# Loads that carry both experts of a pair, a first gather in one piece, and a re-ordered last pair in a one-core mixture-of-experts layer

## Chip, core and metric

The kernel runs on one core of one Trainium2 chip. The metric is device time in microseconds (us) of one execution. The kernel before takes 1322.36 us, the median of three runs (1322.08 to 1322.64).

## What is computed

One encoder layer on 256 tokens of width 2048, all in float32. The first part (an input projection, a gated convolution, a differential attention and an output projection) stays as it is. The second part is a mixture of 32 experts, of which each token uses two of the eight in one group:

```python
def hier_moe(x, w_group, b_group, w_router, b_router, w_gate, w_up, w_down):
    ...
    expert_id = g_idx[:, None] * EXPERTS_PER_GROUP + top_i
    combine = jnp.sum(jax.nn.one_hot(expert_id, N_EXPERTS, dtype=jnp.float32)
                      * (g_w * top_p)[..., None], axis=1)
    out = jnp.zeros_like(t)
    for e in range(N_EXPERTS):
        h = jax.nn.silu(t @ w_gate[e]) * (t @ w_up[e])
        out = out + combine[:, e:e + 1].astype(t.dtype) * (h @ w_down[e])
    return out.reshape(B, S, D)
...
        h = h + jnp.concatenate([y_conv, y_attn], axis=-1) @ w_out[l]
        h = h + hier_moe(rms_norm(h, norm2_g[l]), ...)
```

The gate and up matrices of an expert are 2048 x 512 each, the down matrix is 512 x 2048. The 32 experts hold 403 MB of the 466 MB that the kernel reads from HBM.

## The kernel before

The tokens of an expert are brought together in 64 slots, and two experts make a pair: 16 pairs, `p` = 0 to 15, NP = 16. The helpers below are those of the page's lines.

- `dispatch` (L836) makes the 0/1 matrix `dg` of a pair on VectorE. `gather` (L855) multiplies the tokens `xs` with `dg` on TensorE (L861) for n blocks of 128 features and scales the result into `tT` on VectorE (L863). `tT` has 16 blocks, so a pair takes four gathers of four blocks.
- `gate_up` (L869) multiplies `tT` of one expert with its eight chunks of gate and up weights (L880), into one PSUM bank of the two called "gu"; then comes the silu on ScalarE (L884) and the product `hid` on VectorE (L885). It runs for the one expert of the pair and then for the other (`gate_ups`, L1010).
- `flip_hidden` (L887) turns `hid` into `hT` (TensorE L891, ScalarE L893). `down` (L904) makes 512 output columns of both experts (L909), four times a pair; the four results stay in the PSUM banks called "dn". `flip_weights` (L896) turns `dg` into `dwT`.
- `weigh` (L916) splits a down result into a high and a low part `y` (ScalarE L926, VectorE L927). `scatter` (L931) multiplies `y` with `dwT` (L939) and adds it to the accumulators `acc` (L940). The scatter of pair p-1 stands in the loop of pair p, between the gathers of pair p+1. In the last loop (p = 15) there are no gathers any more, and the scatter of pair 14 stands alone ahead of the downs of pair 15. Behind them each down's scatter and the stores follow.
- A sum in float32 is two passes on TensorE: each matmul with float32 operands has two records in the trace (16 records are eight matmuls).

**Loads.** All weights come through the SP queue in items of 2 MiB, in the order in which they are used: per pair eight items of gate and up (`("gu", p, j)`: two chunks of one expert each) and four of down (`("dn", p, n)`: 512 columns of both experts). There are 192 items. They go round a ring of nine buffers, `E_RING`; two half buffers (`u18`, `u20`) hold the very first item in addition, so ten items are loaded while the first part of the layer runs. Every further load waits until TensorE has used up the item that lies in its buffer: these are the refills, of which there are 182. The last item comes in four DMAs of 512 KB (L1001).

TensorE's order is the order in which the code is written (`manual_schedule`); the other queues' order comes from a scheduler that goes by priorities and dependencies. `nc.values_load(cmaxi)` (L1083) reads the largest token count into a register of every engine, for the branch behind which a slow path for more than 64 tokens would run; no row of that path is in the trace.

## Time and profile before

| | before |
|---|---|
| median of three runs | 1322.36 us |
| profiled execution, own time | 1323.07 us |
| its span, first to last instruction | 1321.2 us |
| TensorE busy | 1238.7 us (94 %) |
| VectorE / ScalarE busy | 513.9 us / 296.5 us |
| mean granted TensorE clock | 0.994 |
| read from HBM | 466.17 MB, 354 GB/s over the span |

The page divides the span into 40 slices of 33 us. In each it gives the engines' busy share in tenths, the DMA engines' share and the rate in GB/s. A row of the chain of waits has the start (us), the length and the operation or the transfer that ended last. A row of the table by windows has the stretch, its length, the busy time of PE, PEld (weight loads), DVE (VectorE), ACT (ScalarE) and POOL with the number of records, then the granted clock, the DMA share and the rate in GB/s. A row of the timeline has the start, the length of the group, the engine, line, operation and shapes, and in brackets the idle time ahead of it and what ended it; SPq is the DMA queue of SP. A row by form has the busy time and the mean of one in ns.

### The profile page before, as it was taken

Reading aid. Unit: us, or ns where it says so; the run is one execution under the profiler, and the core shown is the slowest. Engines: PE = TensorE matmul, PEld = TensorE weight load, DVE = VectorE, ACT = ScalarE, POOL = GpSimd, SP = SyncE. Lnnn points to the kernel's source line nnn. Section 1 sums busy time; section 2 is a strip of 40 time slices with the busy share of each in tenths; the row PEclk is TensorE's granted clock in tenths of the full one; section 3 lists DMA queues with packets and bytes.
Section 4 is the critical chain, followed back from the end, with each engine's and each line's share of the span. In section 5 each row is a group of like instructions: output and inputs, shape, how many; then the busy total and the mean of one; then the engine's idle time right before and its main releaser. Section 6 shows DMA issues by size and latency. Waiting matters only on the chain.

```text
span 1321.2 us, 15090 instructions
## 1 busy us (share of the span) xinstructions
PE 1238.7 (94%) x6263; PEld 701.7 (53%) x6263; DVE 513.9 (39%) x990; ACT 296.5 (22%) x573; POOL 46.5 (4%) x116
## 2 busy tenths in 40 slices
PE   7999999899999999999989898989989898998987
PEld 5887888787874353553525344343525435352522
DVE  6888898997442130330303123030303213030304
ACT  6446647565321010110101101010101100010101
POOL 1001200420000000000000000000000000000000
PEclk9999999999999999999999999999999999999999
DMA  9454554755648999999999999999999999999994
GB/s 385 173 184 168 191 191 141 296 200 209 245 186 360 414 428 428 428 428 427 428 427 428 428 427 428 428 428 427 428 428 427 427 428 428 428 427 428 428 428 177
DMA packets 36010, 469.31 MB, mean 355 GB/s; under 512 B 4064, under 2 KB 4064, under 8 KB 7776
## 3 DMA queue, kind: packets, MB, share of 16 engines
q1 hardware_dynamic: 35648, 467.68, 85.1%
q8 instruction: 51, 0.84, 0.3%
q10 hardware_dynamic: 288, 0.60, 0.1%
q14 instruction: 23, 0.19, 0.0%
HBM read 466.17 MB, written 2.10 MB: 354 GB/s over the span
## 4 chain that ended last, share of the span: by engine, by line
PE 64%; DMA 30%; DVE 2%; ACT 2%; POOL 1%; issue 0%; SPq 0%; DVEq 0%; ACTq 0%
DMA v<-in_w_gu_dram 29%; PE b L909 14%; PE b L880 12%; PE b L861 9%; PE b L714 7%; PE b L713 7%; PE b L712 7%; PE b L939 5%; PE b L497 1%; ACT u L663 1%; ACT t L428 1%; PE b L624 1%; DVE u L664 1%; PE b L891 0%; DMA v<-in_w_in_dram 0%
## 5 line engine op out<-in xcount | busy, mean ns | idle before, releaser
L880 PE MATMUL b<-v,u 128*64 128x512 f32 x2032 | 451.2, 596 | 52.0 <-DMA v<-in_w_gu_dram 52.0
L880 PEld LDWEIGHTS b<-v,u 128*64 128x64 f32 x2032 | 144.0, 137 | 354.1 <-issue 277.6
L885 DVE TENSOR_TENSOR hid<-sil,b 64x512 f32<-64x512 f32 x32 | 21.9, 685 | 551.3 <-ACT sil L884 551.3
L909 PE MATMUL b<-v,hT 128*64 128x512 f32 x1024 | 223.9, 594 | 0.0
L712 PE MATMUL b<-u,v 128*128 128x512 f32 x448 | 179.8, 401 | 9.3 <-ACT u L663 8.6
L714 PE MATMUL b<-u,v 128*128 128x512 f32 x448 | 176.5, 394 | 1.8 <-DVE v L579 1.8
L713 PE MATMUL b<-u,v 128*128 128x512 f32 x448 | 176.2, 393 | 1.1 <-DVE u L664 1.1
L664 DVE TENSOR_TENSOR u<-v,u 128x1024 fp32r<-128x1024 f32 x112 | 137.6, 1229 | 54.8 <-ACT u L663 54.0
L663 ACT ACTIVATE u<-v 128x1024 fp32r<-128x1024 f32 x112 | 119.2, 1065 | 140.4 <-PE b L714 109.7
L884 ACT ACTIVATE sil<-b,sv 64x512 f32<-64x512 f32 x32 | 21.9, 683 | 569.1 <-PE b L880 569.1
L909 PEld LDWEIGHTS b<-v,hT 128*64 128x64 f32 x1024 | 71.9, 137 | 137.0 <-issue 136.4
L861 PEld LDWEIGHTS b<-dg,xs 128*128 128x128 f32 x1024 | 121.3, 192 | 17.5 <-issue 15.0
L861 PE MATMUL b<-dg,xs 128*128 128x128 f32 x1024 | 126.4, 277 | 0.2 <-DVE dg L841 0.2
L712 PEld LDWEIGHTS b<-u,v 128*128 128x128 f32 x448 | 85.3, 190 | 26.3 <-ACT u L663 8.6
L323 DVE SCALAR_TENSOR_TENSOR v<-v,pr 128x255 f32<-128x255 f32 (+14 forms) x240 | 97.1, 464 | 0.0
L714 PEld LDWEIGHTS b<-u,v 128*128 128x128 f32 x448 | 85.0, 190 | 21.0 <-DVE v L579 2.9
L713 PEld LDWEIGHTS b<-u,v 128*128 128x128 f32 x448 | 85.3, 190 | 18.4 <-DVE u L664 1.6
L926 ACT ACTIVATE u<-b,sv 128x512 fp32r<-128x512 f32 (+1 forms) x65 | 44.3, 681 | 223.8 <-PE b L909 191.9
L927 DVE SCALAR_TENSOR_TENSOR u<-b,sv,u 128x512 fp32r<-128x512 f32 (+1 forms) x65 | 48.1, 740 | 100.9 <-ACT u L926 100.9
L939 PE MATMUL b<-u,dwT 128*128 128x512 f32 (+1 forms) x260 | 77.3, 416 | 4.4 <-DVE hid L885 1.5
L863 DVE TENSOR_TENSOR u<-b,g2v 128x512 f32<-128x512 f32 (+1 forms) x65 | 44.4, 684 | 39.0 <-PE b L861 38.5
L939 PEld LDWEIGHTS b<-u,dwT 128*128 128x128 f32 x260 | 43.8, 190 | 16.6 <-issue 4.0
(198 smaller groups left out, 553.7 us busy)
## 6 DMA issues: line engine op xcount, KB each, us to landing
v<-in_w_gu_dram SPq DMA_DIRECT2D x127, 2048.0 KB, 32.6
v<-in_w_dn_dram SPq DMA_DIRECT2D x63, 2048.0 KB, 35.1
v<-in_w_in_dram SPq DMA_DIRECT2D x18, 2048.0 KB, 8.0
v<-in_w_out_dram SPq DMA_DIRECT2D x8, 2048.0 KB, 8.1
v<-in_w_in_dram SPq DMA_DIRECT2D x8, 512.0 KB, 9.2
v<-in_xT_dram SPq DMA_DIRECT2D x4, 512.0 KB, 8.8
xs<-in_x_dram SPq DMA_DIRECT2D x2, 1024.0 KB, 12.0
u<-in_w_gu_dram SPq DMA_DIRECT2D x2, 1024.0 KB, 8.4
```

The lines of the kernel that those rows point to most:

```text
L323: nc.vector.scalar_tensor_tensor(cacc[:, b, d:], hb[:, b, :S - d], ck[:, b, j:j + 1], cacc[:, b, d:], op0=ALU.mult, op1=ALU.add)
L663: nc.scalar.activation(sp[:, 0], w, AF.Copy)
L664: nc.vector.tensor_tensor(sp[:, 1], w, sp[:, 0].bitcast(F32), op=ALU.subtract)
L712: nc.tensor.matmul(o, lh, sp[:, 0, k2], start=first and k2 == 0, stop=False)
L713: nc.tensor.matmul(o, lh, sp[:, 1, k2], start=False, stop=False)
L714: nc.tensor.matmul(o, ll, sp[:, 0, k2], start=False, stop=last and k2 == 1)
L861: nc.tensor.matmul(tv[:, k], xs[:, t, (k0 + k) * 128:(k0 + k + 1) * 128], dg[:, t].rearrange("p i c -> p (i c)"), start=t == 0, stop=t == 1)
L863: nc.vector.tensor_tensor(tT[:, k0:k0 + n], tv, g2v[:, k0:k0 + n, None].to_broadcast([128, n, 2 * C]), op=ALU.mult)
L880: nc.tensor.matmul(gu[h:h + 64], tT[:, kb, i * C:(i + 1) * C], w[:, k2, g], start=kb == 0, stop=kb == KB - 1, skip_group_check=True)
L909: nc.tensor.matmul(ps[64 * i:64 * i + 64], hT[:, f, i], wd[i].rearrange("p (f n) -> p f n", f=4)[:, f], start=f == 0, stop=f == 3, skip_gr ...
L927: nc.vector.scalar_tensor_tensor(y[:, 1, c], ps[:, c], sv[:, 0:1], y[:, 0, c].bitcast(F32), op0=ALU.mult, op1=ALU.subtract)
L939: nc.tensor.matmul(ps[:, :w], dwT[:, t], y[:, k, c], start=k == 0, stop=k == 1)
```

## The change

**Loads.** An item of gate and up now holds one chunk (two blocks of 128 features) of both experts of a pair, where it held two chunks of one expert. There are as many items of the same size, and each is one contiguous piece in HBM as before. What lies in the half buffers `u18` and `u20` is no longer the first item but the fourth down item of pair 0, `("dn", 0, 3)`; the ring starts with the eight gate and up items of pair 0. The first four refills (`HALVES`), and the last gate and up item, come as two DMAs of 1 MiB, one for each expert.

**gate_up** works on both experts in turn, chunk by chunk, into both "gu" banks; the silu and the product of both experts stand behind the last chunk. The first pair's gather stands ahead of it in four pieces of four blocks, where it was in five pieces between the chunks; `combine_weights` (which makes `cmaxi`) follows it on VectorE.

**The last two pairs.** The scatter of pair 14 stands behind chunks 1 to 4 of pair 15's gate and up, in the "tp" banks. The last down item comes in three DMAs (`PIECES`: columns 0 to 255, 256 to 383 and 384 to 511) and is worked off in the same three parts, each with its own down, split, scatter and store. For that the down weights lie in HBM and in the buffer as four blocks of 128 columns, each with its four blocks of 128 rows; a down of 512 columns reads four strips of 128 (`columns`). The stores of the second token half go out on ScalarE's queue.

```diff
-FINE = 1
+PIECES = ((0, 256), (256, 384), (384, 512))
+HALVES = 4
...
         for c in range(8):
-            if before_chunk is not None:
-                before_chunk(c)
...
+            for i in range(2):
+                w = chunk(i, c).rearrange("p (k g f) -> p k g f", g=2, k=2)
+                for k2 in range(2):
+                    kb = 2 * c + k2
+                    for g in range(2):
+                        h = 64 * (g ^ i)
+                        nc.tensor.matmul(gu[i][h:h + 64], tT[:, kb, i * C:(i + 1) * C], w[:, k2, g],
+                                         start=kb == 0, stop=kb == KB - 1, skip_group_check=True)
+            if after_chunk is not None:
+                after_chunk(c)
+        sv = sv()
...
+        for i in range(2):
+            own, other = slice(64 * i, 64 * i + 64), slice(64 - 64 * i, 128 - 64 * i)
+            nc.scalar.activation(sil[other], gu[i][own], AF.Silu, scale=sv[own, 1:2])
+            nc.vector.tensor_tensor(hid[own], sil[other], gu[i][other], op=ALU.mult)
...
+    def columns(w, f, a=0, b=512):
+        return w.rearrange("p (c f n) -> p f c n", c=4, f=4)[:, f, a // 128:b // 128]
...
     def load(x):
...
+        halves = len(E_RING) <= ne < len(E_RING) + HALVES or x == ("gu", NP - 1, 7)
+        t = next_pair()
+        for i in range(2):
+            chunks[2 * p + i, j + 8 * (kind == "dn")] = t[:, i]
+            if halves:
+                nc.sync.dma_start(t[:, i], source(x)[:, i])
+        if not halves:
+            nc.sync.dma_start(t, source(x))
...
+        for t in range(NT):
+            (nc.sync, nc.scalar)[t].dma_start(ov[t][:, ns], acc[t][:, ns])
...
+    def gate_ups(p):
+        def after(c):
+            load_next()
+            if p == NP - 1 and 1 <= c <= 4:
+                scatter(weigh(ys[p - 1, c - 1], svs[p - 1]), dwTs[p - 1], acc, c - 1, use="tp")
+        return gate_up(tT, lambda i, c: chunks[2 * p + i, c], lambda: svs[p], after)
...
+    for g in range(4):
+        gather(dgs[0], tT, 4 * g, 4)
+    combine_weights()
...
-            if p > 0:
+            if 0 < p < NP - 1:
                 scatter(weigh(ys[p - 1, g], svs[p - 1]), dwTs[p - 1], base, g)
...
             ys[p, n] = down(hT, [chunks[2 * p + i, 8 + n] for i in range(2)])
+            if p > 0 or n < 3:
+                load_next()
...
+    parts = [(2, 0, 512)] + [(3, a, b) for a, b in PIECES]
+    for (n0, a0, b0), (n, a, b) in zip(parts, parts[1:]):
...
+        two_parts(y3, ps, svs[p], a, b)
+        scatter(y, dwTs[p], acc, n0, a0, b0)
+        store(n0, a0, b0)
...
+    scatter(y, dwTs[p], acc, *parts[-1])
+    store(*parts[-1])
```

TensorE's order at the first pair, before, from the first gather to the end of the first refillable buffer (`v_3167`, the first of the ring; `u_3181` and `u_3183` are the half buffers; a bank's number follows `b_`):

```order
L861 MATMUL b_3205<-dg,xs 128x128 x4
L861 MATMUL b_3211<-dg,xs 128x128 x4
L880 MATMUL b_3204<-u_3181,u_3194 64x512 x4
L861 MATMUL b_3221<-dg,xs 128x128 x8
L880 MATMUL b_3204<-u_3183,u_3194 64x512 x4
L880 MATMUL b_3204<-v_3167,u_3194 64x512 x4
L861 MATMUL b_3239<-dg,xs 128x128 x8
L880 MATMUL b_3204<-v_3167,u_3194 64x512 x4
```

And now, at the same place (L863 is the gather's, L882 gate_up's line):

```order
L863 MATMUL b_3195<-dg,xs 128x128 x8
L863 MATMUL b_3205<-dg,xs 128x128 x8
L863 MATMUL b_3215<-dg,xs 128x128 x8
L863 MATMUL b_3225<-dg,xs 128x128 x8
L882 MATMUL b_3267<-v_3167,u_3194 64x512 x4
L882 MATMUL b_3268<-v_3167,u_3194 64x512 x4
```

Ahead of the last use of the ring's first buffer stood 24 gather matmuls and 16 of gate and up; now there are 32 and 8, and after the first four of these the buffer's first half is used up.

The SP queue at that time, before, from the last of the ten first loads:

```order
L71 DMA v_3185<-in_w_dn_dram 128x4096
L71 DMA v_3196<-in_w_dn_dram 128x4096
L71 DMA v_3198<-in_w_dn_dram 128x4096
L71 DMA v_3200<-in_w_gu_dram 128x4096
L71 DMA v_3202<-in_w_gu_dram 128x4096
```

And now (L980 are loads of 1 MiB, L982 of 2 MiB):

```order
L982 DMA v_3185<-in_w_gu_dram 128x4096
L1102 TENSOR_LOAD cmaxi
L1102 ISA x2
L980 DMA v_3167<-in_w_dn_dram 128x2048 x2
L980 DMA v_3169<-in_w_dn_dram 128x2048 x2
L980 DMA v_3171<-in_w_gu_dram 128x2048 x2
L980 DMA v_3173<-in_w_gu_dram 128x2048 x2
L982 DMA v_3175<-in_w_gu_dram 128x4096
```

The register load of `cmaxi`, which stood between the last stores, is now ahead of the first refill on this queue.

TensorE at the last pair, before, from the last gate and up item to the first down (`u_3581` is `y`):

```order
L880 MATMUL b_6839<-v_6762,u_6652 64x512 x8
L939 MATMUL b_6877<-u_3581,dwT 128x512 x2
L939 MATMUL b_6881<-u_3581,dwT 128x512 x2
L891 MATMUL b_6885<-ident,hid 128x128 x4
L939 MATMUL b_6894<-u_3581,dwT 128x512 x2
L939 MATMUL b_6898<-u_3581,dwT 128x512 x2
L899 MATMUL b_6902<-ident,dg 128x128 x2
L939 MATMUL b_6909<-u_3581,dwT 128x512 x2
L939 MATMUL b_6913<-u_3581,dwT 128x512 x2
L939 MATMUL b_6919<-u_3581,dwT 128x512 x2
L939 MATMUL b_6923<-u_3581,dwT 128x512 x2
L909 MATMUL b_6927<-v_6773,hT 64x512 x8
```

And now, from the last gate and up item to the first down:

```order
L882 MATMUL b_6603<-v_3179,u_6462 64x512 x4
L882 MATMUL b_6604<-v_3179,u_6462 64x512 x4
L898 MATMUL b_6719<-ident,hid 128x128 x4
L906 MATMUL b_6726<-ident,dg 128x128 x2
L920 MATMUL b_6731<-v_3185,hT 64x512 x8
```

The 16 scatter matmuls of pair 14 are gone from this place; four of them follow each of the chunks 1 to 4.

## Rows read from the trace of the kernel before

**Rows 1.** The page, the span in 40 equal slices: DMA share and rate.

```profile
DMA  9454554755648999999999999999999999999994
GB/s 385 173 184 168 191 191 141 296 200 209 245 186 360 414 428 428 428 428 427 428 427 428 428 427 428 428 428 427 428 428 427 427 428 428 428 427 428 428 428 177
```

**Rows 2.** The chain of waits: two early pairs, and the last pairs.

```profile
473.17 1.98 PE b L861 x16
...
526.59 1.98 PE b L861 x16
...
1189.56 32.66 DMA v<-in_w_gu_dram
...
1248.48 32.69 DMA v<-in_w_gu_dram
1281.21 3.65 PE b L880 x16
```

**Rows 3.** Table by windows, all engines, where the experts' loads begin.

```profile
380.00:382.00 2.00, 2.00 (x20) 2.00 (x19) 1.32 (x7) 1.36 (x2) 0.00 (x0) 1.00 1.00 397
388.00:400.00 12.00, 12.00 (x69) 6.15 (x70) 1.81 (x3) 0.00 (x0) 0.00 (x0) 1.00 0.00 0
400.00:402.00 2.00, 2.00 (x15) 1.17 (x12) 0.00 (x0) 0.00 (x0) 0.00 (x0) 1.00 0.97 205
...
436.00:438.00 2.00, 2.00 (x12) 0.72 (x10) 0.75 (x1) 0.14 (x1) 0.00 (x0) 1.00 0.88 229
438.00:1280.00 842.00, 791.24 (x4096) 358.73 (x4092) 178.62 (x334) 71.22 (x114) 0.00 (x0) 1.00 1.01 428
```

**Rows 4.** Timeline of the SP queue: refills 1, 8 and 20.

```profile
399.37 0.33 SPq L71 DMA_DIRECT2D v<-in_w_dn_dram  x1
...
435.44 0.33 SPq L71 DMA_DIRECT2D v<-in_w_gu_dram  x1
...
488.86 0.33 SPq L71 DMA_DIRECT2D v<-in_w_gu_dram  x1
```

**Rows 5.** Timeline of TensorE, first pairs: gathers, then gate and up.

```profile
386.02 2.02 PE L861 MATMUL b<-dg,xs 128*128 128x128 f32 x16 [0.21 <-DVE dg L841]
...
422.68 3.84 PE L861 MATMUL b<-dg,xs 128*128 128x128 f32 x32
...
445.53 27.64 PE L880 MATMUL b<-v,u 128*64 128x512 f32 x128
```

**Rows 6.** Timeline of TensorE, last pair: the downs.

```profile
1293.51 5.37 PE L909 MATMUL b<-v,hT 128*64 128x512 f32 x24
1298.82 1.20 PE L939 MATMUL b<-u,dwT 128*128 128x512 f32 x4
1299.94 3.65 PE L909 MATMUL b<-v,hT 128*64 128x512 f32 x16
...
1304.66 3.65 PE L909 MATMUL b<-v,hT 128*64 128x512 f32 x16
```

**Rows 7.** Timeline of ScalarE in the last pair.

```profile
1284.91 0.69 ACT L884 ACTIVATE sil<-b,sv 64x512 f32<-64x512 f32 x1 [18.58 <-PE b L880]
...
1288.22 0.60 ACT L893 ACTIVATE hT<-b 128x512 f32<-128x512 f32 x1
```

**Rows 8.** Timeline of VectorE in the last pair, with its last instruction.

```profile
1286.28 0.68 DVE L885 TENSOR_TENSOR hid<-sil,b 64x512 f32<-64x512 f32 x1
...
1315.14 0.42 DVE L940 TENSOR_TENSOR acc<-acc,b 128x256 f32<-128x256 f32 x1 [0.27 <-PE b L939]
```

**Rows 9.** Groups by line and form in the last 11 us.

```profile
L939 PE MATMUL b<-u,dwT 128*128 128x256 f32 x8 | 2.3, 346 | 1.5 <-ACT u L926 0.6 <-DVE u L927 0.4 <-DVE u L940 0.3
...
L927 DVE SCALAR_TENSOR_TENSOR u<-b,sv,u 128x256 fp32r<-128x256 f32 x2 | 1.0, 482 | 1.6 <-ACT u L926 1.6
L926 ACT ACTIVATE u<-b,sv 128x256 fp32r<-128x256 f32 x2 | 0.9, 474 | 4.6 <-PE b L909 4.0 <-DVE u L927 0.6
```

**Rows 10.** Register load of the token count (L1083) on the SP queue.

```profile
L1083 SPq TENSOR_LOAD <-cmaxi x1: 527/527/527, 1310.9 to 1310.9; - x1
```

More of the change, by code (lines that the diff above doesn't have):

```diff
@@ L976, in block_kernel @@
     todo = [x for p in range(NP) for x in [("gu", p, j) for j in range(8)] + [("dn", p, n) for n in range(4)]]
[L978 to L983 removed]
+    late = todo.pop(11)
+    for n, x in enumerate(todo[:len(E_RING)]):
+        if n == 7:
+            for i, u in enumerate((18, 20)):
+                chunks[i, 11] = unit(u, [128, 2048])
+                nc.sync.dma_start(chunks[i, 11], source(late)[:, i])
@@ L984, in block_kernel @@
         load(x)
     todo = todo[len(E_RING):]
-    def load_more(k):
-        k = max(0, min(k, len(todo) - FINE))
-        for x in todo[:k]:
-            load(x)
-        del todo[:k]
-        if len(todo) == FINE:
-            while todo:
-                x = todo.pop(0)
-                t = pair(next_pair(), [128, 2, 2048])
-                for k, key in enumerate(keys_of(x)):
-                    chunks[key] = t[:, k]
-                for f in range(4):
-                    fs = slice(f * 512, f * 512 + 512)
-                    nc.sync.dma_start(t[:, :, fs], source(x)[:, :, fs])
@@ L1003, in store, with load_next @@
-    def store(n, t):
-        ns = slice(n * 512, (n + 1) * 512)
-        nc.sync.dma_start(ov[t][:, ns], acc[t][:, ns])
+    def load_next(*_):
+        if len(todo) > 1:
+            load(todo.pop(0))
+        elif todo:
+            x = todo.pop(0)
+            t = next_pair()
+            for i in range(2):
+                chunks[2 * x[1] + i, 8 + x[2]] = t[:, i]
+            for a, b in PIECES:
+                nc.sync.dma_start(t[:, :, 4 * a:4 * b], source(x)[:, :, 4 * a:4 * b])
+    def store(n, a=0, b=512):
+        ns = slice(n * 512 + a, n * 512 + b)
+        for t in range(NT):
+            (nc.sync, nc.scalar)[t].dma_start(ov[t][:, ns], acc[t][:, ns])
```

135 lines of the change are left out of this document (52 added, 83 removed).

## The prediction, made before the changed kernel was run

> **What bounds the kernel now.** I read the slices of the page first. From the fourteenth slice on the rate is 427 to 428 GB/s and the DMA share 9 tenths or more, up to the last slice [rows 1]. So some 900 us of the span are one stream of expert loads, and what TensorE does meanwhile costs nothing as long as it gives the buffers back in time. The chain of waits says the same: early pairs follow each other in 53.42 us (473.17 to 526.59) with TensorE alone in the chain, late ones in 58.92 us (1189.56 to 1248.48) with a gate and up load as the longest link [rows 2]. TensorE thus has 5.5 us to spare in every pair. An item of 2.097 MB at 428 GB/s takes 4.90 us, and twelve take 58.8, the pair's period. The end is therefore the time at which the stream starts, plus its gaps, plus 182 items, plus what TensorE does behind the last items.
>
> The windows show the gaps. The stream is dry from 388 to 400, and once more by half in 436 to 438 (229 GB/s), never again until 1280 [rows 3]. The first refill is issued at 399.37 [rows 4]; 400 to 402 moves 0.41 MB, as much as a stream that starts at 401.0, so data flow some 1.7 us after an issue. The second gap is of the same kind: seven refills fill 34.3 us, the eighth is issued only at 435.44, when the first down has freed a buffer, and lands by 435.44 + 1.7 + 4.9 = 442.0.
>
> At the other end the last gate and up item releases TensorE at 1281.21 [rows 2], the four down items behind it land by about 1286.1, 1291.0, 1295.9 and 1300.8, and VectorE's last instruction ends at 1315.56 [rows 8]. TensorE is late there, not the loads: the first down starts at 1293.51 [rows 6], though its weights are there at 1286.1. From 1315.56 to the span's end at 1321.2 the last store and the end of the program take 5.6 us, and I leave these as they are.
>
> **The change, part by part. The start of the stream.** Before, 24 gather matmuls and 16 of gate and up stand ahead of the first release; now 32 and 4, because the halves are freed one by one. 32 gather records take 3.84 us with a tail of less than 0.1, and 128 of gate and up 27.64, or 0.215 each [rows 5]. Four gathers from 386.02 take 7.5 us, to 393.5; eight records more take 1.7, so the first half is free at 395.2. SP also has the register load to do ahead of it, which waits for `cmaxi`. The last gather's scaling on VectorE ends about 0.8 us behind the gather, at 394.3, two small operations follow, and the load takes 0.53 us [rows 10] and some 0.2 of checks: 395.5. I take 395.6 for the first issue, 3.8 us earlier than 399.37. TensorE then frees 2 MiB in 3.45 us where the stream needs 4.9, so it doesn't run dry. Eight refills now lie ahead of the first down and not seven, since the eight gate and up buffers are all free by then and the fourth down item sits in the half buffers. They end at 395.6 + 1.7 + 39.2 = 436.5. The four that go in halves have packets of 8 KB; the nearest row, 380 to 382 with such a load under way, has 397 GB/s [rows 3], which would make 8.4 MB 1.5 us longer. Nothing says that they are faster; I take 0.6: 437.1, against 442.0 for the same item before, a gain of 4.9 us.
>
> Is it kept? The ninth refill follows the first down, which I expect 1 us earlier than before: the same instructions, without the switching between gathers and chunks (36.7 us from 386.02 to 422.68 for 7.5 + 27.6 of work and two small matmuls for the scalars [rows 5], some 1.2 us over), less a little for the register scalars behind the last chunk. 434.4 + 1.7 = 436.1 is ahead of 437.1, so the second gap closes. The next narrow place is the twentieth refill, behind the first down of pair 1: before at 488.86 [rows 4], now 487.9 + 1.7 = 489.6, where the nineteenth ends at 437.1 + 11 x 4.9 = 491.0. It holds with 1.4 us; from pair to pair the margin grows by TensorE's 5.5. Were the stream faster, this refill would cap the gain at 6.3. **Front: -4.9 us, from -6.3 to -3.4.**
>
> **The last pair,** in the times of before; 4.9 comes off all of them. Chunks land 4.91 apart, the last at 1281.2 in both. Four scatter matmuls take 1.1 us behind each of the chunks 1 to 4; with 3.45 for a chunk that is 4.5, inside 4.9. Their splits can be made far ahead, since pair 14's down results have been waiting since its downs. TensorE is through with pair 14's downs at about 1251.9 (three of the four are done where the chain goes over to the load at 1248.48 [rows 2], one takes 3.4), when chunks 0 and 1 are there. Eight chunks and four scatters from there end at 1283.9; no chunk comes too late for that, the last half (1281.2) included, and before it was 1284.9. Then silu 0.69, product 0.68, transposes about 0.5 (four records of the gather's size), copy 0.60 [rows 7, 8]: `hT` is ready at 1286.6, because no scatter and no accumulation stands between (before, these pushed the down to 1293.51). The first expert's silu and product lie under the last matmuls. The first down starts at 1286.6, its weights being there, and ends at 1290.1, the second waits for 1291.0, the third for 1295.9; with a scatter in each (4.72 from 1299.94 to 1304.66 [rows 6]) the third ends at 1300.65.
>
> Then come the three parts. 256 columns: half of 3.43, 1.7. 128 columns: no row has 128 moving columns against 64 stationary ones. A quarter of 0.215 a record gives 0.9 for the sixteen, the gather's 0.12 a record (128 columns, but twice the stationary columns) 1.9 [rows 5]; I take 1.3, near the middle, since the stationary columns are half of the gather's. The chain: part a to 1302.4, scatter of the third down 1.1, part b 1.3, scatter of a 0.5, part c 1.3 to 1306.6. For a split of 128 columns I take three quarters of the 256-column rows (0.47 and 0.48 [rows 9]): 0.36 each. With the handing over, `y` of c is there at 1307.5, its scatter takes 0.35 [rows 9], two accumulations of about 0.3: 1308.4. Before it was 1315.56. The stores of the second half go from ScalarE's queue, whose splits never stand behind a store that isn't ready by then; the last two go out side by side, worth nothing here, as they were 1 us apart anyway. The pieces of the last item land by 1301 or a little later, and part c starts at 1305.3. **Tail: -7.1 us.** With small matmuls at 0.9 or 1.9, and half a us of hand-overs either way, -8.3 to -5.0.
>
> **At no cost:** silu and product of both experts behind the last chunk (1.4 us more in a row) lie under the first gather of the next pair, and under TensorE's 5.5 us; without that cover they would cost some 1.4 x 15 = 21 us. Both "gu" banks are held until then, so the first scatter of a pair waits for the second product; that falls under the same gather. The stream's rate stays, as the items are the same size and contiguous.
>
> **Sum:** 4.9 + 7.1 = 12.0 us. The span goes from 1321.2 to 1309.2, the profiled execution from 1323.07 to 1311.1. The median of before lies 0.7 us under its profiled execution: 1322.36 - 12.0 = **1310.4 us**.
>
> **A rule against it.** For 1 MiB loads next to others the one row has 397 GB/s [rows 3], so the halves cost at most 1.5 us by it. The Trainium skill, "DMA: Bandwidth & Descriptors", section "Bandwidth", gives 341 GB/s for single DMAs of 1 MB and 425 at 16 MB, and asks for batches of 1 MiB and more. That would be an estimate of 24.6 us for the four halved items, 5.0 more than 19.6, and the front's gain would be gone. Row and page differ, and those figures are for loads from another queue. It is the first rival.
>
> **The rivals.** First: the front gives nothing. The halves' transfers cost as much as the head start brings, or the stream runs dry again at the twentieth refill because TensorE is later than I think in pair 0 or 1. For it: margins of 1.0 and 1.4 us only, and no row with four halved items in a row. Against: the halves are issued faster than they are served, so that several are under way at once, and 397 GB/s. Time: 1322.4 - 7.1 = 1315.3. Chance 0.12.
>
> Second: the tail is bound by its small steps (three splits of two engines in turn, three scatters, banks that come free late) and gives 3.5 us, not 7.1. For it: before, TensorE already waited 1.5 us in all for the two 256-column parts [rows 9]. Time 1314.0, chance 0.08.
>
> Third, the slower one: the down's moving operand is now four strips of 128 columns, 2 KB apart, where it was one run of 512, and no row shows such a read. The downs are 64 x 0.215 = 13.8 us of a pair's 53.4. TensorE stays hidden until they are 40% (5.5 us) slower; above that it sets the pace in all sixteen pairs: at half speed a pair takes 53.4 + 13.8 = 67.2, 8.4 over the stream's, and the kernel some 1322 + 16 x 8.4 - 12 = 1445. At 50% slower it is 1.4 a pair, about 1333. No row bears on it; I take zero for it, since the columns are as many as before. Chance 0.05.
>
> Fourth: the change doesn't do what it says at the start, because SP's register load (or a scheduler's order behind it) holds the first refill until the first whole item is free, at 397.0 or later. The ending of the eight moves by 1.5 to 3 and so does the whole: about 1312.5. Chance 0.05.
>
> **How the numbers follow.** The forecast has 0.70: 1310.4, with its terms' bounds 1307.7 to 1314.0. The range takes in the first, second and fourth rival and half a us below: 1307.0 to 1315.5; outside lie the slower rival and some of both ends, under 2 in 10. A measurement of this kernel can tell about 0.2%, 2.6 us, from no change, so faster means under 1319.7. All cases but the third lie there: faster 0.93, same 0.02, slower 0.05.
>
> **What would show it.** After: SP's first refill at about 395.6, a DMA rate without a hole in 436 to 438 and around 490, the last gate and up item at TensorE at about 1276 and the first down at 1281.7; last accumulation at about 1303.5. Wrong would be: a rate clearly under 400 in 397 to 420, a register load that ends after 396, a hole at 490, downs longer than 3.5 us each, or matmuls of 128 columns above 0.12 us a record.

## The result

The changed kernel took 1312.93 us (median of 4 runs, 1311.37 to 1314.85) against 1322.5 us of the kernel before beside it: ratio 0.9925, 95% interval 0.9913 to 0.9937. A second set gave 1313.74 us and 0.9926 (0.9913 to 0.9938). The forecast was 1310.4 us, range 1307.0 to 1315.5, faster: right in sign and range, 2.5 us too low. The profiled execution of after took 1314.85 us with a span of 1312.9, so it is the longest of its four; the rows below are to be read with some 2 us of that in mind.

The slices of the page, DMA share and rate, stand against [rows 1]:

```profile
DMA  9444553745658999999999999999999999999996
GB/s 384 185 182 167 190 192 136 291 188 193 254 222 359 427 427 428 428 426 430 427 427 429 427 428 426 428 427 428 427 427 429 426 428 428 426 429 426 428 427 242
```

The same plateau, and a last slice with 242 instead of 177 GB/s: less time without loads at the end. The windows of after (length, busy time of PE, PEld, DVE, ACT and POOL, clock, DMA share, GB/s), against [rows 3]:

```profile
398.00:400.00 2.00, 2.00 (x12) 0.58 (x10) 0.67 (x4) 0.00 (x0) 0.00 (x0) 1.00 0.86 307
400.00:402.00 2.00, 2.00 (x12) 0.72 (x10) 0.00 (x0) 0.00 (x0) 0.00 (x0) 1.00 0.95 336
402.00:404.00 2.00, 2.00 (x12) 0.70 (x10) 0.00 (x0) 0.00 (x0) 0.00 (x0) 1.00 0.99 369
404.00:406.00 2.00, 2.00 (x12) 0.59 (x10) 0.00 (x0) 0.00 (x0) 0.00 (x0) 1.00 1.01 406
436.00:438.00 2.00, 2.00 (x12) 0.72 (x10) 0.00 (x0) 0.00 (x0) 0.00 (x0) 1.00 0.94 401
438.00:1280.00 842.00, 796.49 (x4128) 359.97 (x4125) 185.02 (x344) 72.41 (x116) 0.00 (x0) 1.00 1.01 427
```

The stream now runs in 398 to 400, where it stood still, and 436 to 438 moves 401 instead of 229 GB/s. The SP queue and its register load, against [rows 4, 10] (refills 1, 8, 9 and 20; the load's row gives durations in ns and its start):

```profile
396.81 0.33 SPq L980 DMA_DIRECT2D v<-in_w_dn_dram  x1
...
422.55 0.33 SPq L982 DMA_DIRECT2D v<-in_w_gu_dram  x1
436.35 0.33 SPq L982 DMA_DIRECT2D v<-in_w_gu_dram  x1
...
489.77 0.33 SPq L982 DMA_DIRECT2D v<-in_w_gu_dram  x1
```

```profile
L1102 SPq TENSOR_LOAD <-cmaxi x1: 471/471/471, 395.9 to 395.9; - x1
```

Refill 8 is 13 us earlier than in [rows 4]. TensorE's first pair, against [rows 5]:

```profile
387.50 7.38 PE L863 MATMUL b<-dg,xs 128*128 128x128 f32 x64 [0.36 <-DVE dg L843]
394.81 27.69 PE L882 MATMUL b<-v,u 128*64 128x512 f32 x128
...
432.66 10.52 PE L920 MATMUL b<-v,hT 128*64 128x512 f32 x48
```

The first gather starts 1.5 us later than before (387.50 against 386.02), out of code that the change doesn't touch. At the other end, TensorE in the last pair, against [rows 6], then ScalarE and VectorE, against [rows 7, 8]:

```profile
1270.98 10.84 PE L882 MATMUL b<-v,u 128*64 128x512 f32 x48
...
1284.69 3.65 PE L920 MATMUL b<-v,hT 128*64 128x512 f32 x16 [0.49 <-ACT hT L900]
1289.60 1.94 PE L920 MATMUL b<-v,hT 128*64 128x512 f32 x8 [1.26 <-DMA v<-in_w_dn_dram]
...
1299.24 1.90 PE L1088 MATMUL b<-v,hT 128*64 128x256 f32 x16
1301.06 1.20 PE L947 MATMUL b<-u,dwT 128*128 128x512 f32 x4
1302.19 1.09 PE L1088 MATMUL b<-v,hT 128*64 128x128 f32 x16
...
1305.94 0.80 PE L947 MATMUL b<-u,dwT 128*128 128x128 f32 x4 [0.25 <-DVE u L948]
```

```profile
1281.88 0.68 ACT L890 ACTIVATE sil<-b,sv 64x512 f32<-64x512 f32 x1 [1.04 <-PE b L882]
1284.02 0.60 ACT L900 ACTIVATE hT<-b 128x512 f32<-128x512 f32 x1 [1.46 <-PE b L898]
```

```profile
1306.78 0.29 DVE L948 TENSOR_TENSOR acc<-acc,b 128x128 f32<-128x128 f32 x1
```

Between `hid` and the first down no scatter stands any more. The down begins 2.1 us after the last silu is done, and VectorE ends at 1307.07 instead of 1315.56. The chain of waits now goes through a load up to the second down, which [rows 2] had reached at the 16th layer's last chunk already:

```profile
1255.17 34.29 DMA v<-in_w_dn_dram
1289.60 1.94 PE b L920 x8
```

**Where 8.3 us of the profiled span came from.** I set the records of both traces against each other. The 60th item of 2 MiB has been moved 108.2 us after the first gather, before 113.1: -4.9. From the landing of the last gate and up load to the last sum it is 27.3 us (1279.72 to 1307.07), before 34.4 (1281.16 to 1315.56): -7.1. The late first gather gives +1.5, the program's end +0.2. That makes -10.3; 2 us more were lost between the 60th item and the landing of the last gate and up load, while the rate stayed at 427 GB/s. That is the interesting part of this case.

The trace records 16 landings for each load, which I take for one from each of the 16 DMA engines. The time from the first to the last of the 16 landings of an item (the **lag**) tells how far the slowest engine is behind the quickest; TensorE can start only after the last: the second down's wait ends at 1289.60, the last of its load's 16 landings stands at 1289.5, the first at 1280.5. The table is worked out from the trace's records. The 60th item counts the bytes that all engines together have moved, 60 times 2 MiB since the start. The column behind the lags is the time from the first gather to the last of the 16 landings of the last gate and up load, so it goes by the slowest engine.

```
                  first    60th item  lag near  lag near  gather to   last gate/up  median (runs)  ratio to before,
                  gather   after it   446 us    1270 us   last        load to last                 95% interval
                                                          gate/up     sum
before            386.02   113.1      0.8       6.8       895.1       34.4          1322.50 (4)
after             387.50   108.2      2.6       9.0       892.2       27.3          1312.93 (4)    0.9925 (0.9913-0.9937)
e6_same           387.92   108.2      1.9       7.9       891.3       27.3          1313.74 (5)    0.9926 (0.9913-0.9938)
e1_first_item     387.77   112.7      1.9       7.4       895.5       28.1          1314.36 (5)    0.9935 (0.9923-0.9948)
e1_again          386.62   112.4      0.8       7.0       894.7       27.3          1316.32 (6)    0.9947 (0.9934-0.9960)
e7_no_preload     387.79   113.3      3.2       9.3       897.5       27.4          1316.88 (5)    0.9949 (0.9936-0.9962)
e2_no_halves      386.74   109.3      2.1       8.2       892.5       27.4          1312.13 (4)    0.9913 (0.9899-0.9928)
e5_early_gather   385.31   108.6      0.7       7.3       891.1       27.3          1311.30 (4)    0.9907 (0.9892-0.9921)
e3_scatter_back   385.68   108.4      3.2       9.5       892.8       31.4          1316.71 (6)    0.9956 (0.9943-0.9969)
e4_one_piece      385.78   108.3      3.6       9.8       892.8       28.1          1313.08 (5)    0.9927 (0.9914-0.9939)
e8_more_code      388.26   108.3      2.4       22.2      906.4       27.5          1327.83 (6)    1.0034 (1.0022-1.0046)
v2_late_gathers   384.82   107.0      2.0       6.7       889.0       32.0          1313.74 (5)    0.9931 (0.9917-0.9945)
v3_late_scatter   386.19   108.2      2.0       7.9       891.1       28.7          1314.59 (5)    0.9934 (0.9920-0.9948)
v4_three_pairs    384.50   106.8      2.0       6.8       889.0       29.0          1311.64 (6)    0.9914 (0.9901-0.9927)
```

### The profile page after: what moved, and what is told of

Its sections match the earlier page's. It is cut to its first block, busy times and chain, and to the rows that moved or that the text cites. A ratio compares the mean times of both kernels' runs of the same rounds, so it can differ in the third digit from the quotient of the medians.

```text
span 1312.9 us, 15143 instructions
## 1 busy us (share of the span) xinstructions
PE 1236.6 (94%) x6299; PEld 702.0 (53%) x6299; DVE 514.1 (39%) x992; ACT 296.2 (23%) x574; POOL 48.0 (4%) x116
## 4 chain that ended last, share of the span: by engine, by line
PE 61%; DMA 33%; DVE 2%; ACT 1%; POOL 1%; issue 0%; ACTq 0%; SPq 0%; DVEq 0%
DMA v<-in_w_gu_dram 28%; PE b L882 13%; PE b L920 13%; PE b L863 8%; PE b L716 6%; PE b L714 6%; PE b L715 6%; PE b L947 4%; DMA v<-in_w_dn_dram 3%; DMA v<-in_w_in_dram 1%; PE b L499 1%; ACT u L665 1%; DMA v<-in_xT_dram 1%; ACT t L430 1%; DVE u L666 1%; PE b L626 1%
## 5 line engine op out<-in xcount | busy, mean ns | idle before, releaser
L882 PE MATMUL b<-v,u 128*64 128x512 f32 x2048 | 452.4, 594 | 45.5 <-DMA v<-in_w_gu_dram 45.4
L882 PEld LDWEIGHTS b<-v,u 128*64 128x64 f32 x2048 | 142.9, 137 | 349.6 <-issue 264.2
L920 PE MATMUL b<-v,hT 128*64 128x512 f32 x992 | 217.2, 594 | 1.7 <-DMA v<-in_w_dn_dram 1.3
L863 PEld LDWEIGHTS b<-dg,xs 128*128 128x128 f32 x1024 | 121.1, 192 | 14.8 <-issue 11.9
L863 PE MATMUL b<-dg,xs 128*128 128x128 f32 x1024 | 125.5, 276 | 0.6 <-DVE dg L843 0.4
L947 PE MATMUL b<-u,dwT 128*128 128x512 f32 (+2 forms) x264 | 76.7, 412 | 0.2 <-DVE u L948 0.2
L865 DVE TENSOR_TENSOR u<-b,g2v 128x512 f32<-128x512 f32 x64 | 44.3, 692 | 29.8 <-PE b L863 29.4
L948 DVE TENSOR_TENSOR u<-u,b 128x512 f32<-128x512 f32 (+2 forms) x62 | 41.2, 664 | 30.1 <-PE b L947 30.1
```

Source lines behind the costliest of these rows:

```text
L863: nc.tensor.matmul(tv[:, k], xs[:, t, (k0 + k) * 128:(k0 + k + 1) * 128], dg[:, t].rearrange("p i c -> p (i c)"), start=t == 0, stop=t == 1)
L882: nc.tensor.matmul(gu[i][h:h + 64], tT[:, kb, i * C:(i + 1) * C], w[:, k2, g], start=kb == 0, stop=kb == KB - 1, skip_group_check=True)
L920: nc.tensor.matmul(ps[64 * i:64 * i + 64], hT[:, f, i], columns(wd[i], f), start=f == 0, stop=f == 3, skip_group_check=True)
L947: nc.tensor.matmul(ps[:, :b - a], dwT[:, t], y[:, k, a:b], start=k == 0, stop=k == 1)
```

## The experiments

The theory after the first comparison: the front gave its 4.9 us, the tail its 7.1, and part of the front was given back because the slowest DMA engine is further behind when nothing stops the stream. The rivals: the front gives nothing, since something else sets the time; the tail came from the loads; the 2 us belong to this one execution.

**The changed kernel once more.**

> The changed kernel once more, unaltered, as the base for the runs beside it. Median near 1312.9 us. Two things of its first profile are in doubt. The late start of the expert stage (first gather 387.50 us against 386.02 before): if it belongs to one execution, the first gather stands at another time here, between 386.0 and 387.5, with the half-clock stretch of TensorE elsewhere than at 300 to 340 us; if the change causes it, again 387.5. The lag of the slowest of the 16 DMA engines at the last whole items (9.0 us from first to last landing, against 6.6 to 6.8 before): if it follows from the program's own instruction blocks, 9.0 within 0.5 again; if it differs from execution to execution, anywhere from 6 to 9, and the end of the load stream moves with it.

The late first gather came again (387.92), with the clock at half speed in the same place; but in eight of the others, whose first layer is the same, it stands at 384.5 to 386.7, and one kernel that ran twice (e1_first_item, e1_again) has 387.77 and 386.62. It belongs to the execution, not to the change. The lag was 7.9, between the two cases: it isn't fixed by the program, but it is again above the 6.8 of before.

**The first item in the half buffers again.**

```
-    late = todo.pop(11)
+    late = todo.pop(0)
...
-    hid = gate_up(tT, lambda i, c: chunks[i, c], first_scalars, load_next)
+    hid = gate_up(tT, lambda i, c: chunks[i, c], first_scalars,
+                  lambda c: load_next() if c > 0 else None)
...
-            if p > 0 or n < 3:
-                load_next()
+            load_next()
```

> One part undone: the two half buffers hold the first pair's first item again instead of its fourth down item, so seven refills and not eight lie ahead of the first down. Theory: the eighth refill is issued after the first down (near 436.4 us on the clock of the changed kernel) instead of at 422.6, the loads run dry for 3 to 5 us just before it (window 434 to 438 far under 428 GB/s), and everything behind is one item later: +4.7 us by the median against the changed kernel run beside it (1317.6), bounds +3 to +5.5. Rival, by which the front gives nothing since TensorE or a later refill sets the time: within 1 us of the changed kernel (1312 to 1314).

> The kernel of the first run that undid the front, once more. Its profiled execution lost 4.85 us of load stream at the second gap, as the theory said, but that execution was the slowest of five (1319.0 us) and the median stood only 0.6 us over the changed kernel's. Theory (the stream sets the end, and the execution's own late first layer and the lag of the slowest DMA engine are noise of 2 us to either side): over both sets of runs the ratio to the kernel before lies 2 to 5 us over that of the changed kernel (median 1315.5 to 1318.5 here), and the profile shows the hole before 438 us again. Rival (something behind gives most of the 4.8 us back, so that the front was worth about 1 us): median 1313 to 1314.5 again, in the profile too.

The hole is back. The eighth refill, which now waits for the first down, is issued at 436.63 in the first run (422.55 in after), and the second run's window reads 246 GB/s where after has 401:

```profile
436.63 0.33 SPq L982 DMA_DIRECT2D v<-in_w_gu_dram  x1
```

```profile
436.00:438.00 2.00, 2.00 (x12) 0.72 (x10) 0.75 (x1) 0.17 (x1) 0.00 (x0) 1.00 0.85 246
```

The 60th item came 4.5 and 4.2 us later after the first gather, as the theory says. The medians moved less: 0.9 to 2.1 thousandths, 1.2 to 2.8 us; the first run's (1314.36) lies below the theory's bounds, the second's (1316.32) inside them. Most of the difference is in the table. By the slowest engine the last gate and up load comes 895.5 and 894.7 us behind the first gather, against 892.3 on average in the four kernels with the front of after (after, e6, e3, e4: 891.3 to 892.8). That is 3.2 and 2.4 us, as the lag at the end is 7.0 to 7.4 instead of 7.9 to 9.8. The rest lies within the scatter of the runs of one kernel, 3 to 5 us. So the front is shown in the trace at 4.2 to 4.5 us of stream, of which the end gets 2.4 to 3.2.

**No preloaded item.** Left out of the after kernel: the half buffers' item; it comes as a normal refill.

```
-    late = todo.pop(11)
...
-        if n == 7:
-            for i, u in enumerate((18, 20)):
-                chunks[i, 11] = unit(u, [128, 2048])
-                nc.sync.dma_start(chunks[i, 11], source(late)[:, i])
```

> No half-buffer item at all: nine items of 2 MiB are loaded ahead of the expert stage instead of ten, the rest of the order is the changed kernel's, and its refills come at the same times. The load stream then has one item more to move behind the first refill, with no hole that the other kernel lacks: 2 MiB at 428 GB/s is 4.9 us. Theory (the stream from the first refill to the last item sets the end): +4.9 us against the changed kernel, 1318 by the median, bounds 1316.5 to 1319. Rival (TensorE sets it, and an item more is caught up): within 1 us of the changed kernel (1312 to 1314.5).

One item more in the stream, without a hole (434 GB/s in 436 to 438): the 60th item came 5.1 us later, the lag stayed high (3.2 and 9.3), and the time rose by 3.0 (by the ratios) to 4.0 us. The stream sets the end; a rival by which TensorE does is out. That a whole item costs 5 us in the trace, by the slowest engine too (897.5 against 892.3), but rather 3.5 in the medians stays open.

**Whole first refills.** `HALVES = 0` instead of 4.

> One part undone: the first four refills go as one load of 2 MiB each and not as two halves, so the first is issued one half chunk of TensorE work (1.7 us) later. Theory: the stream starts 1.7 us later, and the slower start of the halves (307 to 336 GB/s in the first 4 us, some 0.9 us lost) is saved: +0.4 to +1.7 us in the window 398 to 438, hardly to be told in the median (1313 to 1315). Rival, from the rule on the rate of 1 MiB loads: the halves slow the stream while they last, and without them the end is 3 to 5 us earlier (1308 to 1310).

Windows of this kernel (columns as above); 400 to 402 stands at 393 instead of 336 GB/s:

```profile
400.00:402.00 2.00, 2.00 (x12) 0.72 (x10) 0.00 (x0) 0.00 (x0) 0.00 (x0) 1.00 0.94 393
402.00:404.00 2.00, 2.00 (x12) 0.60 (x10) 0.00 (x0) 0.00 (x0) 0.00 (x0) 1.00 0.95 410
```

The first refill left 11.0 us after the first gather instead of 9.3, 1.7 later as foreseen, and the 60th item came 1.1 later. So the halves give 1.7 us of head start and cost 0.6 to 0.7 of rate in their first microseconds. The medians can't tell this much: they went the other way, 0.8 to 1.6 us, to 1312.13, below the theory's 1313. The rival of 3 to 5 us is out.

**Two gathers ahead of the first chunk.**

```
-    for g in range(4):
+    for g in range(2):
         gather(dgs[0], tT, 4 * g, 4)
     combine_weights()
+    def then(c):
+        load_next()
+        if c in (1, 3):
+            gather(dgs[0], tT, 4 * (c // 2 + 2), 4)
```

> One part varied: only two of the four gathers lie ahead of the first chunk, the others between chunks 2 and 3 and 4 and 5, and the combine weights come before the third; the first half chunk is free some 3.7 us earlier, and so the first refill. Theory: the ninth refill waits for the first down, which TensorE reaches at the same time as before (its work in the stretch is the same), so the stream runs dry for about 3.5 us before 438 us and nothing is won: within 1 us of the changed kernel (1312 to 1314). Rival (the time of the first refill alone counts): the whole 3.7 us come off, 1309.5.

Its SP queue and the window behind:

```profile
391.06 0.33 SPq L980 DMA_DIRECT2D v<-in_w_dn_dram  x1
...
434.86 0.33 SPq L982 DMA_DIRECT2D v<-in_w_gu_dram  x1
```

```profile
430.00:438.00 8.00, 8.00 (x45) 3.50 (x45) 0.91 (x3) 0.00 (x0) 0.00 (x0) 1.00 0.60 211
```

The first refill is 3.6 us earlier behind the first gather (5.75 against 9.31), the stream runs dry for half of 430 to 438, and the 60th item is not earlier (108.6): the ninth refill, which waits for the first down, decides. That is the prediction's argument for eight refills ahead of the first down. Yet the median is 1.6 to 2.4 us lower. This kernel has the hole and, with it, a lag of 0.7 us behind it and 7.3 at the end, at the same stream. The hole let the slow engines catch up, as in before and e1_again (from 2.0 to 0.8 and from 1.8 to 0.7). But by the slowest engine the last gate and up load is here at 891.1, in after at 892.2 and in e6 at 891.3, so in the trace this is worth 0.2 to 1.1 us; the rest of the profiled gain is a first gather that is 2.2 to 2.6 us earlier in this execution. That the kernel is faster than after isn't shown: the intervals overlap.

**The scatter back in its place.**

```
-            if 0 < p < NP - 1:
+            if 0 < p:
                 scatter(weigh(ys[p - 1, g], svs[p - 1]), dwTs[p - 1], base, g)
...
-            if p == NP - 1 and 1 <= c <= 4:
-                scatter(weigh(ys[p - 1, c - 1], svs[p - 1]), dwTs[p - 1], acc, c - 1, use="tp")
```

> One part undone: the 15th pair's scatter lies again between the 16th pair's first layer and its downs. Theory: four scatters of four F32R matmuls (1.13 us each) come back between the end of the first layer and the first down, less what the wait for silu, product and hT (2.0 us) covers of them; the first down starts near 1287.5 instead of 1284.7, and as TensorE works without a gap from there to the end, the end is later by 2.5 to 5.5 us: 1317 by the median, bounds 1315.4 to 1318.4. Rival, by which the end is set by the last load (last piece lands 1300.1) and the scatter only fills TensorE's waits for loads: within 1 us of the changed kernel.

TensorE behind the last chunk (which ends at 1280.6):

```profile
1282.74 0.73 PE L947 MATMUL b<-u,dwT 128*128 128x512 f32 x2 [1.49 <-DVE hid L891]
...
1288.35 0.96 PE L947 MATMUL b<-u,dwT 128*128 128x512 f32 x3 [0.69 <-DVE u L929]
1289.24 5.37 PE L920 MATMUL b<-v,hT 128*64 128x512 f32 x24
```

The first down starts 10.7 us after the last gate and up landing (1278.52), in after 5.0. From that landing to the last sum it is 31.4 instead of 27.3: the move is worth 4.1 us, by the medians 3.0 to 3.8. The loads don't set this stretch, and the rival is out. Four scatters are 4.5 us of matmuls; that the down moves by more, 5.7, is the waiting for weighing and sums that stands between them.

**The last columns in one piece.** `PIECES = ((0, 512),)`.

> One part undone: the last 512 columns come in one load and are worked in one piece. Theory A, from the trace of the changed kernel: TensorE works without a gap from 1291.5 on, so an earlier piece of the last load can't start earlier work; what the three parts save is only the chain behind the last down (weighing 0.5 us and scatter and sum of 128 instead of 512 columns), +0.7 to +1.8 us without them. Rival B, the prediction's: the parts are worth more, since the last piece alone stands behind the last landing: +2 to +4 us. Rival C: smaller steps cost as much as they save, -0.5 to +0.5.

```profile
1298.87 3.65 PE L1088 MATMUL b<-v,hT 128*64 128x512 f32 x16 [0.51 <-DMA v<-in_w_dn_dram]
1302.45 1.20 PE L947 MATMUL b<-u,dwT 128*128 128x512 f32 x4
1304.06 1.90 PE L947 MATMUL b<-u,dwT 128*128 128x512 f32 x4 [0.41 <-DVE u L948]
```

TensorE waits 0.51 us for the piece, and the stretch from the last gate and up landing to the end is 28.1 instead of 27.3 us. Three parts bring 0.7 us in the trace (28.06 against 27.34), the lower end of theory A, and nothing that the medians show (1313.08 against 1313.74). The prediction had counted them into its tail without a price of their own.

**More instructions.**

```
+            if c == 0:
+                nc.gpsimd.tensor_copy(spare, svs[p - 1][:, 0:1])
+            for _ in range(36):
+                nc.gpsimd.memset(spare, 0.0)
```

> The changed kernel with 288 writes of one element per partition by GpSimd added to each pair's first layer from the second pair on (4320 in all), work that nobody waits for; what it adds that matters is instructions, 4320 x 64 bytes, some 17 fetches of 16 KB on the DMA engines beside the 51 there were. Theory (each such fetch holds one of the 16 DMA engines, and the loads queued on it lag by 1 to 1.5 us from then on): the lag from first to last landing of the last whole items grows from 8 to 9.8 us to 10 to 13, and the end is 1 to 3.5 us later (1314.5 to 1317). Rival (the lag comes from elsewhere): lag 8 to 9.8 us and the time of the changed kernel (1312 to 1314).

Fetches of instructions are packets of their own on the 16 engines; the DMA part of its page (packets, MB, share of 16 engines), and windows:

```profile
q8 instruction: 51, 0.84, 0.3%
q14 instruction: 58, 0.47, 0.1%
```

```profile
440.00:800.00 360.00, 346.78 (x1798) 156.71 (x1796) 77.60 (x146) 31.21 (x50) 209.62 (x2109) 1.00 1.01 427
...
1280.00:1300.00 20.00, 18.58 (x84) 6.32 (x80) 4.13 (x7) 1.37 (x2) 0.00 (x0) 1.00 0.79 323
```

After has 51 of 16 KB on q8 and 22 of 8 KB on q14, so there are 36 more of 8 KB, 0.3 MB in all. They cost 14 us. The rate stays at 427 GB/s, the 60th item comes at the same time, but the lag grows from 2.4 us near 446 us to 22.2 near 1270: 15 of the 16 landings of an item lie within 7.0 us, the last comes 15 us behind the fifteenth. Between 497 and 1231 us it rises from 2.5 to 23.7 us in 31 steps, each at one of the 8 KB packets, while the first fifteen landings spread to 7.8 us, about as in after (6.9). The records name no engine, but this means that the added fetches fell to one of the sixteen and held it about 0.7 us each (21.2 / 31). The last gate and up load lands at 1294.68 instead of 1279.72, the slice behind 1280 moves only 323 GB/s, with one engine still busy. The theory's mechanism is shown, at four times the upper end that I expected, since I had spread the fetches over several engines. The Trainium skill, "Runtime: NRT & Kernel Launch", section "Instruction fetch mechanics", calls the cost of such a fetch mostly hidden. What it is for the engine that runs the instructions, this run doesn't show; for a load stream that fills all 16 DMA engines it isn't hidden, and the measurement decides.

**Versions that go on from here.** The first two have two gathers ahead of the layer and two inside in every pair, the second also every scatter in the next layer; the third has the late gathers in three pairs only. All work the last pair's second down item in two halves. The third's diff, in its main lines:

```
-            if not last:
+            if not last and (g < 2 or p + 1 > 2):
                 gather(dgs[p + 1], tT, 4 * g, 4)
...
+            if p <= 2 and c in (1, 3):
+                gather(dgs[p], tT, 4 * (c // 2 + 2), 4)
...
+CUTS = {1: ((0, 256), (256, 512)), 2: ((0, 512),), 3: PIECES}
```

> A version that goes on from the changed kernel: for every pair only two gathers lie ahead of the first layer and two inside it (after chunks 2 and 4), so that the first down of the first pair, which frees the ninth refill, comes 3.8 us earlier on TensorE; and of the last pair the second down item comes and is worked in two halves of 256 columns, since TensorE waited 1.26 us for it. Theory (the ninth refill was the cap of the run with the early gather, then the first down of the second pair near 485 us): the stream is 2.3 to 3.3 us earlier against that run (item 60 at 490.6 to 491.7 us at the same start), the lag of the slowest DMA engine is not reset by a hole and costs 0.5 to 2 us of it, and the halves give 1 us: 1308.5 by the median, bounds 1307 to 1311. Rival (TensorE, with 56 to 57 us of work a pair against 58.8 us of loads, sets it once the loads are ahead): within 1 us of 1311.3.

> The same, and every pair's scatter lies in the next pair's first layer, as the change does it for the 15th alone; the downs of each pair then start 4.5 us earlier on TensorE, and the refills that they free too. Theory: as the version above, and without the narrow place at the first down of the second pair, 0 to 1 us less: 1308 by the median, bounds 1306.5 to 1311. Rival: the scatters' weighing and sums on ScalarE and VectorE come into the way of the gathers' copies inside the layer and hold TensorE, up to 2 us more than the version above.

> The version with the late gathers, but for the first three pairs alone; the others have their four gathers ahead of the layer as in the changed kernel. With late gathers in every pair the last load of the 16th layer landed 5.9 us earlier than in the changed kernel (1273.84 against 1279.72 us), but TensorE ended that layer at 1280.2, only 1.6 us earlier, since it had 36.7 us of work in a layer of 34.3 us of loads. Theory: with nothing but the 15th pair's scatter in the last layer TensorE keeps up (layer ends 2 us after its last landing, near 1276), and from there to the end 22 to 23 us of work lie ahead as before: last sum near 1302, 1308.5 by the median, bounds 1307 to 1310.5. Rival (TensorE was late before the last layer already, from the downs of the 15th pair): 1311 to 1314.

The last layer of v2 (first fence) and v4 (second), TensorE:

```profile
1269.71 10.52 PE L883 MATMUL b<-v,u 128*64 128x512 f32 x48
1281.74 0.66 PE L899 MATMUL b<-ident,hid 128*128 128x128 f32 x4 [1.51 <-DVE hid L892]
```

```profile
1230.29 13.96 PE L921 MATMUL b<-v,hT 128*64 128x512 f32 x64
1244.08 7.04 PE L883 MATMUL b<-v,u 128*64 128x512 f32 x32
...
1266.31 10.52 PE L883 MATMUL b<-v,u 128*64 128x512 f32 x48
...
1279.68 5.33 PE L921 MATMUL b<-v,hT 128*64 128x512 f32 x16 [0.47 <-ACT hT L901]
```

The stream gained about half of what I said. In v2 the 60th item is 1.2 us earlier than in after and 1.6 earlier than in e5 (theory: 2.3 to 3.3), in v4 1.4 and 1.8. It runs dry a second time, in front of the refill that the second pair's first down frees; windows of v2:

```profile
486.00:488.00 2.00, 2.00 (x12) 0.60 (x10) 0.33 (x1) 0.69 (x1) 0.00 (x0) 1.00 0.59 205
488.00:490.00 2.00, 2.00 (x12) 0.72 (x10) 0.42 (x1) 0.00 (x0) 0.00 (x0) 1.00 0.88 229
```

None of the three theories held. v2 gave nothing (0.9931), nor did v3 (0.9934, 1314.59, where its rival had put it), and v4 gave 1.3 to 2.1 us by the medians, with an interval that overlaps that of after (0.9914, 1311.64, in its rival's range). In v3 the second pair's layer, with the scatter in it, takes 37.4 us instead of 31.8 in v2; the stream falls to 287 and 344 GB/s from 474 to 478, and the 60th item is no earlier than in after. TensorE waits there only twice 0.3 us, so by these rows it is the scatter's matmuls rather than the rival's weighing.

In v2 the last gate and up load lands at 1273.84 and TensorE ends the layer at 1280.2. In v4 the layer starts at 1244.08, nearly 5 us after its first item landed, because the 15th pair's gathers, scatters and downs lie ahead of it without a gap; it ends 3.4 us after its last landing (1273.48), not 2. With the last gate and up load 6 us earlier than in after (3.2 of them counted from the first gather), TensorE is the bound in the last two pairs. A second loss is the clock: the first down's 16 records take 5.33 us in v4 and 5.35 in v2, where after has 3.65, because 3.4 us of the tail lie at the lower clock (1.2 GHz), behind the waits for `hid` and `hT` (1.51 and 0.47 us) that after has too. In e1_first_item such a stretch costs 0.8 us (28.1 against 27.3 in e1_again). The late layer and the clock together make the time from the last landing to the last sum long in v2 and v4. e5 and v4 have the lowest medians, and neither can be told from the other; their intervals overlap with that of after.

## Why the prediction held, and where its sum was off

**The start of the stream: right.** First refill 9.3 us after the first gather, forecast 9.6. Eight refills ahead of the first down, 401 GB/s in 436 to 438, no hole near 490, and 4.9 us gained at the 60th item: the forecast of 4.9. The halves cost 0.6 to 0.7, where I took 0.6 between 0 and 1.5. The rival by the rule on 1 MB loads is out: the windows show 307 to 406 GB/s only while the stream starts, and whole loads begin at 393 themselves. The rival with the register load came close: the load and its checks end at 396.72 and the refill leaves at 396.81, so SP was ready with hardly anything to spare.

Two signs that were to show an error did come, in part: the rate lies under 400 for the first 6 us of the stream (307, 336 and 369 GB/s) and above it from there on, and the register load ends at 396.4, later than 396, of which the late first gather makes 1.5 us. The 60th item's 4.9 came all the same.

**The tail: right in its sum, and its largest term is shown.** -7.1 from landing to last sum, forecast -7.1. The scatter's move is 4.1 of it by experiment. By the traces of e3 and before, 1.6 more come from the last gate and up load in halves (the last chunk ends 2.1 us after the landing instead of 3.7), and 1.4 from downs, scatters and sums in another cut. The 16 records of 128 columns took 1.02 us, where I had 0.9 to 1.9 and took 1.3. The strips cost nothing: the downs take 594 ns a record as before, so the slower rival is out. The wait for the second down's load is there, 1.26 us, and TensorE then works without one until the last scatter.

**What failed: "The end is therefore the time at which the stream starts, plus its gaps, plus 182 items, plus what TensorE does behind the last items."** That step takes the stream as one queue. It is sixteen, and the end hangs on the slowest. The gap that the change closes was worth 4.9 us to the mean engine, but less to the slowest one, which had arrived late at it and used part of it to catch up: in before the lag is 2.0 us just ahead of the gap and 0.8 behind it, in after 2.6 and stays 2.6. By the last of its landings the eighth refill comes 57.0 us behind the first gather in before and 53.8 in after, a gain of 3.2; at the last gate and up load it is 2.9 (895.1 and 892.2), and 2.8 on average over the four kernels with this front. With 2.8 in place of the front's 4.9 the forecast would have been 1312.5 us, against 1312.93. One us of this varies from execution to execution, since e6, the same kernel, has 891.3.

From 446 to 1270 us the lag grows by 5.5 to 6.6 in all kernels of the table but e8, v2 and v4. In these last two the second hole first takes it from 1.9 to 0.8 and from 1.8 to 0.7, and from there it grows by 5.9 and 6.1. The kernels whose only hole lies before 438 us (before, e5, e1_again) end with a lag of 6.8 to 7.3, those without (after, e6, e2, e3, e4, e7) with 7.9 to 9.8; e1_first_item lies between, with a lag of 1.9 behind its hole and 7.4 at the end.

The packets of instructions that every kernel has account for this growth. In after the lag stands still except for four steps, each in the load that is under way when a 16 KB packet of instructions starts:

```
packet starts (us)   597         809         1018        1234
lag before, after    2.6, 4.2    4.2, 5.7    5.8, 7.3    7.4, 9.0
```

Between two steps lie seven more such packets that don't move the last landing. e2, e3, e4 and e7 show the same four steps. In before, the largest steps are of 0.9 to 1.2 us, also at such packets (453, 647, 866 and 1074 us). That added packets make such a lag, e8 shows by experiment; that the ones that were there do it, the times of the steps show, without a run that leaves them out.

What remains open: why the medians of e7 rise by less than its trace says, and why only every eighth of the packets moves the last landing.

## What to carry to other kernels

A stream that fills all DMA engines ends with its slowest engine. Here a short hole cost less than its length, since the slow engines used it to catch up; so price a gap that is to be closed by the engine that lands last, and look at first and last landing of an item, not at GB/s. Once the stream is ahead by more than TensorE's slack in the last stages, moving loads earlier brings little (v2, v4), and what counts is the work behind the last landing: taking 4.5 us of matmuls out of it gave 4.1 us. Instructions in the stream's time aren't free, even on an engine for which nobody waits.

## What was unexpected

36 fetches of 8 KB of instructions made the kernel 14 us longer, at the same mean rate, by holding back one DMA engine's landings.

TensorE's clock falls to half in the first layer in some executions and not in others, after the same waits. One matmul of the same place in after and in e3_scatter_back, with idle times of 0.69 and 1.41 us ahead in both:

```profile
303.46 0.63 PE L714 MATMUL b<-u,v 128*128 128x512 f32 x1
```

```profile
303.08 0.39 PE L714 MATMUL b<-u,v 128*128 128x512 f32 x1
```

In after the granted clock of 300 to 320 us is 0.91 and a stretch of 3.4 us lies at the lower level (1.2 GHz); in e3 it is 1.00. With that stretch the first gather came at 387.5 to 388.3 us (after, e6, e1_first_item, e7, e8), without it at 384.5 to 386.7. One or two microseconds between single executions of this kernel are thus no effect of a change in the experts' part.
